# Conditioning sums as background steps, and the last layer's gates early

## The chip, the cores and the metric

The kernel runs on one core of a Trainium2 chip. TensorE (PE) multiplies matrices, VectorE (DVE), ScalarE (ACT) and GpSimd (POOL) work element by element, and SyncE (SP) issues the DMA transfers. The metric is the time of one launch in microseconds on the device, as the median of several runs. Before the change it is 1941.36 us.

## The reference

A first block of two layers works on 256 tokens `x` and 256 context tokens, each of width 1024; a second block (FFN, attention, FFN, twice) follows and isn't touched. In the first block each layer's conditioning comes from one vector per unit, `c` for the tokens and `c_ctx` for the context:

```python
def modulation(cond, w, b):
    m = jax.nn.silu(cond) @ w + b
    return jnp.split(m, 3, axis=-1)
...
        sh, sc, gt = modulation(c, ada_w[l], ada_b[l])
        shc, scc, gtc = modulation(c_ctx, ada_w[l], ada_b[l])
        h = rms_norm(x, norm_pre[l]) * (1.0 + sc[:, None]) + sh[:, None]
        hc = rms_norm(xc, norm_pre[l]) * (1.0 + scc) + shc

        z = h @ w_in[l]
        ...
        out = merge_branches(z, (y_a, y_b, y_c), w_branch[l], w_out[l])
        x_new = x + gt[:, None] * rms_norm(out, norm_post[l])
```

So a layer needs two vectors of 1024 at its start (shift and scale, the `mod` of the kernel) and one at its end (the gate `gt`). Each is a product of one row of 1024 with a matrix 1024 x 1024. `merge_branches` multiplies three branches (attention, a long convolution, a gated MLP) by gates and by `w_branch`, adds them, and multiplies the sum by `w_out`. The last layer updates only `x`.

## The kernel before

**Matmuls.** Every fp32 product is three matmuls of halves: ScalarE writes the rounded upper half `hi`, VectorE subtracts and writes the lower half `lo` (`split`, L109), and `mm3` (lines L138 to L140) or `mm3_T` (L214 to L216) adds hi x hi, hi x lo and lo x hi in a PSUM bank. Weights come in raw blocks of 1 MB, are split in pieces of 128 x 1024, and stand in a ring of four `hi` and four `lo` tiles (`wload`). `lin` makes products by token block, `linT` the transposed ones; the four banks of the tag `mm` take both.

**Conditioning.** `cond_cols(l, j, nu)` makes 512 of the 3072 conditioning numbers of a layer: it loads four blocks of 128 x 1024 of the transposed matrix `ada_t` (512 KB each) into tiles of the weight ring, and for each block and unit one `tensor_tensor_reduce` of VectorE (L350, called CUSTOM_DVE_ANT_0 in the trace and ISA in the order) multiplies it by the row of `crow` and adds along it; a small read of the accumulator follows. With two units a group of 512 has eight such reduces. L353 adds the bias. `ada_mod` (j = 0 to 3) writes the shift and scale of a layer, `ada_gate` (j = 4, 5) transposes the sums on TensorE (`tr<-ident,cond`, L222, four for each unit) and multiplies by `norm_post` (L373).

**The order of the work.** Instructions run in the order of the program on each engine, with priorities that move some ahead (`tc.high_priority`, `tc.issue_after`). Work of long latency (filters, convolution, attention heads) is written as generators in the list `bg`; `tick(ns)` inside the matmul loops runs one step of the first when the nanoseconds that the steps before asked for by their `yield` have passed, and `drain()` runs all that is left.

**A layer.** After the products of `w_in` come three merges, each in two halves of 512 columns: `merge(1)`, `merge(2)`, `merge(0)`. Each half forms its selection `sg`, pops one entry of `hooks`, then multiplies by `w_branch` and evacuates (`wb_evac`, L868 and L869). In layer 0 the six hooks are the four groups of layer 1's modulation (into `mod1`) and the two of layer 0's gate (into `gt`); in layer 1 the first four are empty and the last two are its own gate. `drain()` stands before `merge(2)`. A layer ends with `tail`: the product with `w_out` in two halves n of 512 columns. In layer 0 all four token blocks of half 0 come first, in layer 1 both halves of one token block. `ev` squares on ScalarE (L922) into `y` in the slot `s45`, multiplies by the gate on VectorE (L923), and after half 1 adds the normed result to the residual (L927). Then the next layer's, or FFN's, norm and transposes follow (L1041 for the scaling after layer 1).

Tiles with a tag have a fixed number of buffers; a new one waits until the readers of the old one are done. `slot(tag, ...)` has one buffer, `st` four, the ring's `hi` and `lo` four each.

Of the kernel before, what the change touches and what calls it, by code (L numbers as in the profile page):

```python
# [22 lines left out]
GAP = 2600.0  # L23
# [9 lines left out]
def model(ctx: ExitStack, tc: tile.TileContext, I, COL, out, dump=None):  # L33
# [193 lines left out]
    def rsqrt(a, b, eps, tag="rstd"):  # L227

        r = pool.tile([128, 1], F32, name=tag, tag=tag, bufs=6)
# [39 lines left out]
    def first():  # L269
# [70 lines left out]
        def cond_cols(l, j, nu):  # L340

            d = small(8, "cond").rearrange("p (b u) -> p b u", u=2)[:, :, :nu]
            for b in range(4):
                tag = ("hi", "lo")[b % 2]
                wt = wp.tile([128, 1024], F32, name=tag, tag=tag, bufs=4)
                n = (j * 4 + b) * 128
                SP.dma_start(wt, I["ada_t"][l][n:n + 128, :])
                for u in range(nu):
                    junk = pool.tile([128, 1024], BF16, name="w2", tag="w2", bufs=4)
                    DVE.tensor_tensor_reduce(junk, wt, crow[:, u, :], scale=0.5, scalar=0.0, op0=OP.mult, op1=OP.add,  # L350
                                             accum_out=d[:, b, u:u + 1])
            bias = col("ada_b", l)[:, j * 4:j * 4 + 4].unsqueeze(2).to_broadcast([128, 4, nu])
# [3 lines left out]
        def ada_mod(l, j, mod):  # L356
            d = cond_cols(l, j, 2)
            m = mod[:, j // 2, (j % 2) * 4:(j % 2) * 4 + 4, :]
            if j < 2:
                DVE.tensor_copy(m, d)  # L360
            else:
                g = col("norm_pre", l)[:, (j % 2) * 4:(j % 2) * 4 + 4]
                DVE.scalar_tensor_tensor(m, d, 1.0, g.unsqueeze(2).to_broadcast([128, 4, 2]), op0=OP.add, op1=OP.mult)

        def ada_gate(l, j, gt):

            nu = gt.shape[1]
            d = cond_cols(l, j, nu)
            npb = w2()
            SP.dma_start(npb, I["norm_post"][l:l + 1, (j - 4) * 512:(j - 3) * 512].partition_broadcast(128))  # L370
            for u in range(nu):
                ps = transpose4([d[:, b, u:u + 1].to_broadcast([128, 128]) for b in range(4)])
                DVE.tensor_tensor(gt[:, u, (j - 4) * 512:(j - 3) * 512], ps.rearrange("p a b -> p (a b)"), npb, op=OP.mult)  # L373
# [164 lines left out]
        def layer(l, hs, last, hooks, mid=None):  # L538

            W = I["w_in"][l]  # L540
            nu = 1 if last else 2
            T = 256 * nu
# [38 lines left out]
            def spectra():  # L581
# [3 lines left out]
                uT = slot("mg", [128, nu, 2, 2, 512], F32R)  # L585
# [188 lines left out]
            bg.append(heads())  # L774
# [43 lines left out]
            room = slot("mg", [128, 4, T + 128])  # L818
# [26 lines left out]
            mg = slot("mg", [128, 12 if last else 8, T])  # L845
# [49 lines left out]
            drain()  # L895
# [12 lines left out]
            merge(0, gh, gl, False, True)  # L908
# [74 lines left out]
        def later_rows():  # L983
            cond_rows()
            yield 0.0
        bg.append(later_rows())

        def mid0():
            rawalloc.extend(held)
# [451 lines left out]
```

## Time and profile before

| | us |
|---|---|
| median of 3 runs (lowest, highest) | 1941.36 (1939.37, 1943.46) |
| the profiled execution | 1942.45 |
| its span in the trace | 1940.3 |
| TensorE busy | 1900.5 (98%) |
| VectorE busy | 1234.5 (64%) |
| ScalarE busy | 973.4 (50%) |

The span is the stretch that the trace covers, and the profiled execution's time is a little longer. Busy time counts only instructions at work, so TensorE's 98% says that 40 us of the span are not covered by a matmul. [...]

### The profile page before, as it was taken

How to read it: one execution, taken by the hardware profiler on the slowest of the kernel's cores; microseconds unless marked ns; L12 is line 12 of the kernel's file. 1: busy time of each engine (PE TensorE's matmuls, PEld its weight loads, DVE VectorE, ACT ScalarE, POOL GpSimd, SP SyncE). 2: the span in 40 equal slices, each digit the busy share in tenths (PEclk: the TensorE clock that was granted, in tenths of full speed). 3: DMA queues.
4: the chain of work that ended last, by engine and by line, in shares of the span. 5: the costliest groups of instructions: out<-in, count | busy, mean ns of one | idle time of the engine just before them, and what ended most of it. 6: DMA issues, size and time to landing. Idle time of an engine off the chain costs nothing.

```text
span 1940.3 us, 27986 instructions
## 1 busy us (share of the span) xinstructions
PE 1900.5 (98%) x11280; PEld 1641.9 (85%) x11280; DVE 1234.5 (64%) x1862; ACT 973.4 (50%) x1536; POOL 81.0 (4%) x103
## 2 busy tenths in 40 slices
PE   6999999999999999999899999999999999999998
PEld 4788788778788888998799877799889988779996
DVE  4755667775877857657555578655565556875554
ACT  5534355552345457644444457644454445765443
POOL 0010100011000001010000000000000000000000
PEclk9999999999999999999899999999999999999999
DMA  8432323334552444457455554555655555454544
GB/s 292 156 110 77 100 79 131 117 114 150 185 186 93 145 138 134 146 179 280 167 177 172 185 177 138 174 192 172 197 192 186 163 187 175 149 195 152 180 158 141
DMA packets 155056, 312.29 MB, mean 161 GB/s; under 512 B 6126, under 2 KB 15920, under 8 KB 154800
## 3 DMA queue, kind: packets, MB, share of 16 engines
q1 hardware_dynamic: 153776, 306.33, 48.0%
q0 software_dynamic: 1152, 4.19, 0.7%
q8 instruction: 88, 1.44, 0.3%
q14 instruction: 40, 0.33, 0.0%
HBM read 309.45 MB, written 1.05 MB: 160 GB/s over the span
## 4 chain that ended last, share of the span: by engine, by line
PE 50%; DVE 2%; DMA 1%; ACT 1%; issue 0%; POOL 0%; POOLq 0%; ACTq 0%; DVEq 0%
PE mm L140 8%; PE mm L139 8%; PE mm L138 8%; PE mm L215 7%; PE mm L216 7%; PE mm L214 7%; PE tr L222 2%; DVE lo L110 1%; DMA raw<-in_ffn_w_gate 1%; PE po L1229 1%; PE aux L1196 0%; PE aux L1197 0%; ACT hi L110 0%; DMA raw<-in_w_out 0%; PE po L222 0%
## 5 line engine op out<-in xcount | busy, mean ns | idle before, releaser
L110 DVE TENSOR_TENSOR lo<-raw,hi 128x1024 fp32r<-128x1024 f32 (+1 forms) x484 | 575.2, 1193 | 455.0 <-ACT hi L110 449.6
L110 ACT ACTIVATE hi<-raw 128x1024 fp32r<-128x1024 f32 (+1 forms) x484 | 495.6, 1030 | 591.5 <-PE mm L215 307.1
L214 PE MATMUL mm<-H,hi 128*128 128x256 f32 (+1 forms) x2064 | 631.6, 306 | 2.7 <-ACT H L110 2.7
L215 PE MATMUL mm<-H,hi 128*128 128x256 f32 (+1 forms) x2064 | 629.1, 305 | 1.0 <-DVE H L110 1.0
L216 PE MATMUL mm<-H,lo 128*128 128x256 f32 (+1 forms) x2064 | 628.2, 304 | 0.0
L214 PEld LDWEIGHTS mm<-H,hi 128*128 128x128 f32 x2064 | 394.6, 191 | 20.8 <-ACT H L110 3.0
L215 PEld LDWEIGHTS mm<-H,hi 128*128 128x128 f32 x2064 | 394.8, 191 | 18.7 <-DVE H L110 1.9
L216 PEld LDWEIGHTS mm<-H,lo 128*128 128x128 f32 x2064 | 394.7, 191 | 16.7 <-issue 0.8
L138 PE MATMUL mm<-hi,H 128*128 128x512 f32 x576 | 228.4, 397 | 0.0
L140 PE MATMUL mm<-hi,H 128*128 128x512 f32 x576 | 226.7, 394 | 0.4 <-DVE H L110 0.4
L139 PE MATMUL mm<-lo,H 128*128 128x512 f32 x576 | 226.6, 394 | 0.0
L140 PEld LDWEIGHTS mm<-hi,H 128*128 128x128 f32 x576 | 108.9, 189 | 23.5 <-DVE H L110 1.1
L138 PEld LDWEIGHTS mm<-hi,H 128*128 128x128 f32 x576 | 108.9, 189 | 22.7 <-ACT pm L561 0.8
L139 PEld LDWEIGHTS mm<-lo,H 128*128 128x128 f32 x576 | 109.1, 189 | 22.2 <-issue 0.9
L138 PE MATMUL mm<-hi,s 128*128 128x512 f32 x192 | 75.4, 392 | 0.0
L139 PE MATMUL mm<-lo,s 128*128 128x512 f32 x192 | 75.3, 392 | 0.0
L140 PE MATMUL mm<-hi,s 128*128 128x512 f32 x192 | 75.0, 391 | 0.0
L138 PE MATMUL mm<-hi,mg 128*128 128x512 f32 x160 | 62.7, 392 | 0.0
L139 PE MATMUL mm<-lo,mg 128*128 128x512 f32 x160 | 62.6, 391 | 0.0
L140 PE MATMUL mm<-hi,mg 128*128 128x512 f32 x160 | 62.2, 391 | 0.0
L234 POOL TENSOR_TENSOR rstdb<-rstdb,mhalf 128x1 f32<-128x1 f32 x22 | 12.1, 548 | 1040.1 <-DVE rstdb L233 1040.1
L216 PE MATMUL mm<-s,lo 128*128 128x512 f32 (+1 forms) x128 | 47.1, 368 | 0.6 <-DVE lo L110 0.6
(387 smaller groups left out, 2410.9 us busy)
## 6 DMA issues: line engine op xcount, KB each, us to landing
raw<-in_w_in SPq DMA_DIRECT2D x68, 1024.0 KB, 5.3
raw<-in_ffn_w_gate SPq DMA_DIRECT2D x40, 1024.0 KB, 5.2
raw<-in_ffn_w_up SPq DMA_DIRECT2D x40, 1024.0 KB, 5.1
raw<-in_ffn_w_down SPq DMA_DIRECT2D x36, 1024.0 KB, 5.1
raw<-in_w_branch SPq DMA_DIRECT2D x12, 1024.0 KB, 5.1
raw<-in_a_w_qkv SPq DMA_DIRECT2D x12, 1024.0 KB, 5.2
hi<-in_ada_t SPq DMA_DIRECT2D x16, 512.0 KB, 3.8
lo<-in_ada_t SPq DMA_DIRECT2D x16, 512.0 KB, 5.6
```

Source lines behind the costliest of these rows:

```text
L110: last_split[:] = ACT.activation(hi, src, AF.Copy), DVE.tensor_tensor(lo, src, r32(hi), op=OP.subtract)
L138: PE.matmul(o, lhsT=xh, rhs=hi, start=start, stop=False)
L139: PE.matmul(o, lhsT=xh, rhs=lo, start=False, stop=False)
L140: last_mm[0] = PE.matmul(o, lhsT=xl, rhs=hi, start=False, stop=stop)
L214: PE.matmul(o, lhsT=wh, rhs=xh, start=start, stop=False, skip_group_check=skip)
L215: PE.matmul(o, lhsT=wh, rhs=xl, start=False, stop=False, skip_group_check=skip)
L216: last_mm[0] = PE.matmul(o, lhsT=wl, rhs=xh, start=False, stop=stop, skip_group_check=skip)
L222: PE.transpose(ps[:, i * 128:(i + 1) * 128], s, ident)
L234: powers.append(POOL.tensor_tensor(r, r, mhalf[:, :1], op=OP.pow))
L1229: PE.matmul(po[64 * m:64 * m + 64, i, :], lhsT=v[hf][:, b, (2 * i + m) * 64:(2 * i + m + 1) * 64], rhs=pT[t][:, i, m * (t + 1) + b, :], st ...
```

## The change

The conditioning functions become generators that yield after each block, and get their buffers from a function `place` in place of the ring. In layer 0 the rows of `crow` and the modulation of layer 1 are a background item behind the attention heads, in buffers of `st`; the gate of layer 0 is added to the background in the fifth hook, in four buffers of a tile in slot `s45`. Before `merge(2)` only the heads are run to their end; what is left is drained after `merge(0)`. In layer 1 the gate is a background item from the layer's start, in three buffers of the slot `mg`; its result stands in the fourth quarter of `mg` and is copied to its slot in the fifth hook. Line numbers of what follows grow by up to 21: L868, L869, L922, L923, L927 and L1041 become L881, L882, L937, L938, L942 and L1062, the reduce is L349 and the gate's product L376.

```diff
--- before.py
+++ after.py
@@ -226,7 +226,7 @@
 
     def rsqrt(a, b, eps, tag="rstd"):
 
-        r = pool.tile([128, 1], F32, name=tag, tag=tag, bufs=6)
+        r = pool.tile([128, 1], F32, name=tag, tag=tag, bufs=8 if tag == "rstdb" else 6)
         if b is None:
             DVE.tensor_scalar(r, a, eps, None, op0=OP.add)
         else:
@@ -337,40 +337,43 @@
                 ACT.activation(t, c, AF.Tanh, scale=0.5)
                 DVE.scalar_tensor_tensor(c, t, 1.0, c, op0=OP.add, op1=OP.mult)
 
-        def cond_cols(l, j, nu):
+        def cond_cols(l, j, nu, place):
 
             d = small(8, "cond").rearrange("p (b u) -> p b u", u=2)[:, :, :nu]
             for b in range(4):
-                tag = ("hi", "lo")[b % 2]
-                wt = wp.tile([128, 1024], F32, name=tag, tag=tag, bufs=4)
+                wt = place()
                 n = (j * 4 + b) * 128
                 SP.dma_start(wt, I["ada_t"][l][n:n + 128, :])
                 for u in range(nu):
                     junk = pool.tile([128, 1024], BF16, name="w2", tag="w2", bufs=4)
                     DVE.tensor_tensor_reduce(junk, wt, crow[:, u, :], scale=0.5, scalar=0.0, op0=OP.mult, op1=OP.add,
                                              accum_out=d[:, b, u:u + 1])
+                yield 2000.0 * nu
             bias = col("ada_b", l)[:, j * 4:j * 4 + 4].unsqueeze(2).to_broadcast([128, 4, nu])
             DVE.tensor_tensor(d, d, bias, op=OP.add)
             return d
 
-        def ada_mod(l, j, mod):
-            d = cond_cols(l, j, 2)
-            m = mod[:, j // 2, (j % 2) * 4:(j % 2) * 4 + 4, :]
-            if j < 2:
-                DVE.tensor_copy(m, d)
-            else:
-                g = col("norm_pre", l)[:, (j % 2) * 4:(j % 2) * 4 + 4]
-                DVE.scalar_tensor_tensor(m, d, 1.0, g.unsqueeze(2).to_broadcast([128, 4, 2]), op0=OP.add, op1=OP.mult)
-
-        def ada_gate(l, j, gt):
+        def ada_mod(l, mod, place):
+            for j in range(4):
+                d = yield from cond_cols(l, j, 2, place)
+                m = mod[:, j // 2, (j % 2) * 4:(j % 2) * 4 + 4, :]
+                if j < 2:
+                    DVE.tensor_copy(m, d)
+                else:
+                    g = col("norm_pre", l)[:, (j % 2) * 4:(j % 2) * 4 + 4]
+                    DVE.scalar_tensor_tensor(m, d, 1.0, g.unsqueeze(2).to_broadcast([128, 4, 2]), op0=OP.add, op1=OP.mult)
+
+        def ada_gate(l, gt, place):
 
             nu = gt.shape[1]
-            d = cond_cols(l, j, nu)
-            npb = w2()
-            SP.dma_start(npb, I["norm_post"][l:l + 1, (j - 4) * 512:(j - 3) * 512].partition_broadcast(128))
-            for u in range(nu):
-                ps = transpose4([d[:, b, u:u + 1].to_broadcast([128, 128]) for b in range(4)])
-                DVE.tensor_tensor(gt[:, u, (j - 4) * 512:(j - 3) * 512], ps.rearrange("p a b -> p (a b)"), npb, op=OP.mult)
+            for j in (4, 5):
+                d = yield from cond_cols(l, j, nu, place)
+                npb = w2()
+                SP.dma_start(npb, I["norm_post"][l:l + 1, (j - 4) * 512:(j - 3) * 512].partition_broadcast(128))
+                yield GAP
+                for u in range(nu):
+                    ps = transpose4([d[:, b, u:u + 1].to_broadcast([128, 128]) for b in range(4)])
+                    DVE.tensor_tensor(gt[:, u, (j - 4) * 512:(j - 3) * 512], ps.rearrange("p a b -> p (a b)"), npb, op=OP.mult)
 
         def reduced_sin(a, n, ps, b, f):
 
@@ -535,10 +538,17 @@
 
         spec = []
 
-        def layer(l, hs, last, hooks, mid=None):
+        def layer(l, hs, last, hooks, mid=None, beside=None):
 
             W = I["w_in"][l]
             nu = 1 if last else 2
+
+            def mgslot(shape):
+                if not last:
+                    return slot("mg", shape)
+                names = "abcd"[:len(shape) - 1]
+                return mgx[0][:, :math.prod(shape[1:])].rearrange(
+                    f"p ({' '.join(names)}) -> p {' '.join(names)}", **dict(zip(names, shape[1:])))
             T = 256 * nu
             movs = [(0, 256, unit_T(hs[0]))] if last else [(0, 512, lambda kb: (H[:, :, 0, kb, :], H[:, :, 1, kb, :]))]
             toks = [unit_tok(h, t) for h in hs[:nu] for t in range(2)]
@@ -582,7 +592,7 @@
 
 
                 D, G, Ksp, K256, rk = spec
-                uT = slot("mg", [128, nu, 2, 2, 512], F32R)
+                uT = slot("s8" if last else "mg", [128, nu, 2, 2, 512], F32R)
                 eos = []
                 for u in range(nu):
                     front, back = u_[:, :, u * 256:u * 256 + 128], u_[:, :, u * 256 + 128:(u + 1) * 256][:, :, ::-1]
@@ -771,7 +781,10 @@
                         yield gap
                     if n + 1 < len(units) and units[n + 1][0] != units[n][0]:
                         yield from stack(units[n + 1][0])
-            bg.append(heads())
+            heads_ = heads()
+            bg.append(heads_)
+            if beside:
+                bg.append(beside())
 
 
             if not last:
@@ -815,7 +828,7 @@
                 DVE.scalar_tensor_tensor(g, g, r, lnb, op0=OP.mult, op1=OP.add)
             lin(W, 8, CGM + 512, 512, toks, gv_evac)
 
-            room = slot("mg", [128, 4, T + 128])
+            room = mgslot([128, 4, T + 128])
             uu, bt = room[:, :, :T], room[:, :, T:]
             for i in range(2):
                 SP.dma_start(bt[i * 64:(i + 1) * 64], I["gm_bs"][l].rearrange("(b i) q -> i b q", i=2)[i:i + 1].partition_broadcast(64))
@@ -842,7 +855,7 @@
             zT(CGC, gc_evac)
 
 
-            mg = slot("mg", [128, 12 if last else 8, T])
+            mg = mgslot([128, 12 if last else 8, T])
             later = []
 
             def merge(i, gh, gl, first_, last_):
@@ -892,7 +905,8 @@
             for b in range(4):
                 split(gh[:, b, :], gl[:, b, :], gB[:, b, :])
             merge(1, gh, gl, True, False)
-            drain()
+            while heads_ in bg:
+                step()
             gh, gl = gpair(1)
             for b in range(4):
                 split(*[g[:, b, :].rearrange("p (t q) -> p t q", q=128) for g in (gh, gl)], vb[:, b])
@@ -906,6 +920,7 @@
             for b in range(4):
                 split(gh[:, b, :], gl[:, b, :], on[0][:, b, :])
             merge(0, gh, gl, False, True)
+            drain()
             return [H[:, u] for u in range(nu)]
 
         def tail(l, hm, gt, res, done):
@@ -980,11 +995,6 @@
         modulate(xh[1], mod0, 1, hs[1], 0)
         bg.append(hyena_filter(0))
 
-        def later_rows():
-            cond_rows()
-            yield 0.0
-        bg.append(later_rows())
-
         def mid0():
             rawalloc.extend(held)
             raws = [rawload(I["ada_w"][0], k0, 4, j * 512, 512) for j in (1, 3) for k0 in (0, 4)]
@@ -997,15 +1007,21 @@
                 modulate(xh[u], mod0, u, hs[u], 4)
         mid = mid0, mid1, [(u * 256, 256, unit_T(h)) for u, h in enumerate(hs)]
         rope = pool.tile([128, 2, 2, 64], F32, name="rope", tag="rope")
-        gt = []
-
-        def gt0(j):
-            if j == 4:
-                list(hyena_filter(1))
-                gt.append(slot("s2", [128, 2, 1024]))
-            ada_gate(0, j, gt[0])
-        hooks = [lambda j=j: ada_mod(1, j, mod1) for j in range(4)] + [lambda j=j: gt0(j) for j in (4, 5)]
-        hm = layer(0, hs, False, hooks, mid)
+        gt, mgx = [], []
+
+        def beside0():
+            cond_rows()
+            yield 3 * GAP
+            yield from ada_mod(1, mod1, lambda: st([128, 1024], F32))
+
+        def gt0():
+            list(hyena_filter(1))
+            gt.append(slot("s2", [128, 2, 1024]))
+            room = slot("s45", [128, 4, 1024])
+            places = iter([room[:, i, :] for i in range(4)] * 2)
+            bg.append(ada_gate(0, gt[0], lambda: next(places)))
+        hooks = [lambda: None] * 4 + [gt0]
+        hm = layer(0, hs, False, hooks, mid, beside0)
         xs = xtile()
         SP.dma_start(xs, xin)
         res = [xs, slot("s7", [128, 2, 1024])]
@@ -1018,12 +1034,17 @@
         dump("xs0", xs)
         gt.clear()
 
-        def gt1(j):
-            if j == 4:
-                gt.append(slot("s2", [128, 1, 1024]))
-            ada_gate(1, j, gt[0])
-        hooks = [lambda: None] * 4 + [lambda j=j: gt1(j) for j in (4, 5)]
-        hm = layer(1, hs, True, hooks)
+
+        mgx.append(slot("mg", [128, 4096]))
+        early_gt = mgx[0][:, 3072:].rearrange("p (u d) -> p u d", u=1)
+        room = mgx[0].rearrange("p (i k) -> p i k", k=1024)
+        places1 = iter([room[:, i % 3, :] for i in range(8)])
+        bg.append(ada_gate(1, early_gt, lambda: next(places1)))
+
+        def gt1():
+            gt.append(slot("s2", [128, 1, 1024]))
+            ACT.activation(gt[0], early_gt, AF.Copy)
+        hm = layer(1, hs, True, [lambda: None] * 4 + [gt1])
         g1 = slot("s8", [128, 1024])
         SP.dma_start(g1, I["ffn1_norm_2"][0:1].partition_broadcast(128))
         then = norm_to_h(xs, g1)
```

**VectorE at layer 0's end.** The rows go from the last evacuations of `merge(0)` to w_out's first. `lo`, `wl`, `mg` and the numbered `s` written by L110 are lower halves of weights, `H` those of the merged rows, `mm` is a PSUM bank. Before:

```order
L868 SCALAR_TENSOR_TENSOR s_4290<-s_4290,mm 128x512
L869 TENSOR_TENSOR mg<-mg,s_4290 128x512 x2
L110 TENSOR_TENSOR lo<-raw,hi 128x1024
L110 TENSOR_TENSOR H<-mg,H 128x256 x7
L110 TENSOR_TENSOR mg<-raw,mg 128x1024 x2
L110 TENSOR_TENSOR s_4567<-raw,s_4567 128x1024
L110 TENSOR_TENSOR wl<-raw,wh 128x1024
L110 TENSOR_TENSOR lo<-raw,hi 128x1024 x3
L923 TENSOR_TENSOR s_4565<-mm,s_4179 128x512 x4
```

Now the beginning of the same stretch, from the last L881:

```order
L881 SCALAR_TENSOR_TENSOR s_4222<-s_4222,mm 128x512
L110 TENSOR_TENSOR lo<-raw,hi 128x1024
L882 TENSOR_TENSOR mg<-mg,s_4222 128x512
L110 TENSOR_TENSOR H<-mg,H 128x256 x8
L353 TENSOR_TENSOR cond<-cond,cols 128x8
L349 ISA w_4266,cond<-st,crow 128x1024
L349 ISA cond 128x1
L110 TENSOR_TENSOR mg<-raw,mg 128x1024 x2
L110 TENSOR_TENSOR s_4560<-raw,s_4560 128x1024
L110 TENSOR_TENSOR wl<-raw,wh 128x1024
L364 SCALAR_TENSOR_TENSOR mod<-cond,cols 128x8
L349 ISA w_4268,cond<-st,crow 128x1024
```

and its end, up to the first evacuations of w_out (here `s_4139` is the tile of the gate's blocks and `s_4138` the gate):

```order
L349 ISA w_4531,cond<-s_4139,crow 128x1024
L349 ISA cond 128x1
L349 ISA w_4533,cond<-s_4139,crow 128x1024
L349 ISA cond 128x1
L353 TENSOR_TENSOR cond<-cond,cols 128x8
L938 TENSOR_TENSOR s_4558<-mm,s_4138 128x512 x4
L376 TENSOR_TENSOR s_4138<-tr,w_4536 128x512 x2
```

From L881 to the first L938 there are 24 reduces now (8 for the modulation, 16 for the gate), nine lower halves of weights, eight of `H` and two gate products; before, no reduce stands there.

**TensorE at the same place.** The transposes of the gate's sums are `tr<-ident,cond`. Before they stand among the products of `w_branch`, four at a time:

```order
L215 MATMUL mm<-s_3916,hi 128x512
L222 MATMUL tr<-ident,cond 128x128 x4
L216 MATMUL mm<-s_3915,lo 128x512
L214 MATMUL mm<-s_3915,hi 128x512
L215 MATMUL mm<-s_3916,hi 128x512
L216 MATMUL mm<-s_3915,lo 128x512
```

Now they stand between w_out's half 0 (weights `hi`, `lo`) and its half 1 (weights in `mg`):

```order
L138 MATMUL mm<-hi,H 128x512
L139 MATMUL mm<-lo,H 128x512
L140 MATMUL mm<-hi,H 128x512
L222 MATMUL tr<-ident,cond 128x128 x12
L138 MATMUL mm<-mg,H 128x512
L139 MATMUL mm<-mg,H 128x512
L140 MATMUL mm<-mg,H 128x512
```

Twelve of the sixteen transposes moved to this place; the last four come eight products later.

**VectorE at layer 1's end.** `s_8076` (now `s_8061`) is `y`, `xs` the residual. Before:

```order
L923 TENSOR_TENSOR s_8076<-mm,s_7763 128x512
L110 TENSOR_TENSOR lo<-raw,hi 128x1024 x2
L923 TENSOR_TENSOR s_8076<-mm,s_7763 128x512
L233 SCALAR_TENSOR_TENSOR rstd<-small 128x1
L927 SCALAR_TENSOR_TENSOR xs<-s_8076,rstd,xs 128x512
L110 TENSOR_TENSOR lo<-raw,hi 128x1024 x2
L923 TENSOR_TENSOR s_8076<-mm,s_7763 128x512 x2
L233 SCALAR_TENSOR_TENSOR rstd<-small 128x1
L927 SCALAR_TENSOR_TENSOR xs<-s_8076,rstd,xs 128x512 x3
```

Now:

```order
L938 TENSOR_TENSOR s_8061<-mm,s_7799 128x512 x2
L233 SCALAR_TENSOR_TENSOR rstd<-small 128x1
L942 SCALAR_TENSOR_TENSOR xs<-s_8061,rstd,xs 128x512
L110 TENSOR_TENSOR lo<-raw,hi 128x1024 x4
L942 SCALAR_TENSOR_TENSOR xs<-s_8061,rstd,xs 128x512
L938 TENSOR_TENSOR s_8061<-mm,s_7799 128x512
L233 SCALAR_TENSOR_TENSOR rstdb<-small 128x1
L1062 SCALAR_TENSOR_TENSOR w_8167<-xs,rstdb,s_8057 128x512
L1062 SCALAR_TENSOR_TENSOR w_8168<-xs,rstdb,s_8057 128x512
L938 TENSOR_TENSOR s_8061<-mm,s_7799 128x512
```

The second half of token block 0's residual and its two scalings (L1062) moved ahead of the last evacuation of token block 1.

## Rows read from the trace of the kernel before

**Rows 1.** The page: span, busy time, and loads of ada_t with us to landing.
```profile
span 1940.3 us, 27986 instructions
...
PE 1900.5 (98%) x11280; PEld 1641.9 (85%) x11280; DVE 1234.5 (64%) x1862; ACT 973.4 (50%) x1536; POOL 81.0 (4%) x103
...
hi<-in_ada_t SPq DMA_DIRECT2D x16, 512.0 KB, 3.8
lo<-in_ada_t SPq DMA_DIRECT2D x16, 512.0 KB, 5.6
```
**Rows 2.** Busy time by stretch: stretch, its us, busy us of each engine, clock.
```profile
core 0: us, PE busy (x) PEld busy (x) DVE busy (x) ACT busy (x) POOL busy (x), PEclk, DMA share, GB/s
567.34:588.94 21.60, 21.60 (x97) 17.86 (x96) 15.38 (x22) 11.29 (x18) 0.00 (x0) 1.00 0.70 231
...
613.22:665.00 51.78, 51.40 (x329) 46.55 (x328) 41.44 (x78) 28.91 (x54) 3.65 (x4) 1.00 0.37 120
...
880.00:904.00 24.00, 22.59 (x187) 22.13 (x186) 21.35 (x31) 10.12 (x12) 0.00 (x0) 1.00 0.80 286
904.00:927.62 23.62, 22.69 (x96) 17.40 (x94) 17.64 (x22) 12.72 (x20) 0.55 (x1) 1.00 0.75 244
927.62:933.19 5.57, 0.00 (x1) 0.01 (x1) 4.33 (x10) 2.79 (x8) 1.54 (x2) 0.83 1.00 358
933.19:942.82 9.63, 9.25 (x28) 6.95 (x29) 3.29 (x6) 1.20 (x2) 0.55 (x1) 0.57 0.04 14
942.82:952.00 9.18, 9.18 (x46) 7.72 (x45) 4.79 (x5) 7.37 (x9) 0.00 (x0) 1.00 0.05 8
```
**Rows 3.** VectorE's groups in w_out's half 0 of layer 0: busy us, mean ns.
```profile
L110 DVE TENSOR_TENSOR lo<-raw,hi 128x1024 fp32r<-128x1024 f32 x4 | 4.8, 1222 | 3.9 <-ACT hi L110 3.9
L110 DVE TENSOR_TENSOR H<-mg,H 128x256 fp32r<-128x256 f32 x8 | 2.8, 417 | 0.0
...
L923 DVE TENSOR_TENSOR s<-mm,s 128x512 f32<-128x512 f32 x3 | 2.0, 685 | 0.2 <-ACT s L922 0.2
```
**Rows 4.** TensorE's timeline, halves 0 and 1 of w_out: start us, us, instruction.
```profile
588.71 0.39 PE L140 MATMUL mm<-hi,H 128*128 128x512 f32 x1
588.94 0.39 PE L138 MATMUL mm<-mg,H 128*128 128x512 f32 x1
```
**Rows 5.** VectorE's timeline, the last evacuation of layer 0's last merge.
```profile
567.40 0.68 DVE L868 SCALAR_TENSOR_TENSOR s<-s,mm 128x512 f32<-128x512 f32 x1
```
**Rows 6.** VectorE's timeline, reduces of layer 1's gate.
```profile
893.03 1.23 DVE L350 CUSTOM_DVE_ANT_0 w<-hi,crow 128x1024 bf16<-128x1024 f32 x1 [1.41 <-DMA hi<-in_ada_t]
...
894.30 1.23 DVE L350 CUSTOM_DVE_ANT_0 w<-lo,crow 128x1024 bf16<-128x1024 f32 x1
...
895.45 2.36 DVE L110 TENSOR_TENSOR lo<-raw,hi 128x1024 fp32r<-128x1024 f32 x2
897.72 1.22 DVE L350 CUSTOM_DVE_ANT_0 w<-hi,crow 128x1024 bf16<-128x1024 f32 x1
...
898.87 1.22 DVE L350 CUSTOM_DVE_ANT_0 w<-lo,crow 128x1024 bf16<-128x1024 f32 x1
```
**Rows 7.** TensorE's waits from 870 to 960: us in total, times, longest.
```profile
PE tr L222 <- DVE w L1041: 5.6, 1, 5.6
PE tr L222 <- DVE cond L353: 0.8, 1, 0.8
```
**Rows 8.** TensorE's timeline, products behind the hole at layer 1's end.
```profile
937.19 0.63 PE L138 MATMUL mm<-hi,H 128*128 128x512 f32 x1
...
941.46 0.43 PE L139 MATMUL mm<-lo,H 128*128 128x512 f32 x1
```
**Rows 9.** VectorE's timeline, layer 1's end: evacuations and residual halves.
```profile
927.56 1.51 DVE L923 TENSOR_TENSOR s<-mm,s 128x512 f32<-128x512 f32 x2
...
929.05 0.74 DVE L927 SCALAR_TENSOR_TENSOR xs<-s,rstd,xs 128x512 f32<-128x512 f32 x1
```
**Rows 10.** ScalarE's timeline, a square of w_out's result.
```profile
921.69 0.58 ACT L922 ACTIVATE s<-mm 128x512 f32<-128x512 f32 x1
```

## The prediction

> **What bounds the kernel now.** I read the page's busy part first: TensorE is busy 1900.5 of 1940.3 us and VectorE two thirds of that, so a change of VectorE's work pays or costs only where TensorE stands still for it [rows 1]. Then I read busy time stretch by stretch for the five places the change touches [rows 2]. In layer 0's w_out stage (567.34 to 588.94, the products of output half 0) TensorE is busy 21.60 of 21.60 us and VectorE only 15.38. Layer 1's opening (613.22 to 665.00) leaves VectorE 10.3 us free. Layer 1's last merge and its w_out lose 1.41 and 0.93 us. [...] TensorE's waits name the causes: 5.6 us for VectorE's normed rows, 0.8 us for the gate's sums [rows 7].
>
> **Layer 0: the reduces meet the end of the layer.** Before, layer 0's 48 reduces (24 blocks of ada_t, two units each) were done in the hooks, ahead of the last merge's evacuations; the order has the last of them ahead of the row of L868. Now they are background steps behind the attention heads, two per step, and the rest is drained after merge(0). In VectorE's new order 24 of the 48 stand between the merge's last evacuation (L881) and w_out's first (L938). TensorE can't go round them: 12 transposes of gate sums stand between its two halves of w_out, and the last four of these need the sum (L353) that stands right behind reduce 24. So half 1 waits for that whole queue.
>
> Its start and its content: the last product of the merge is out when VectorE starts L868 at 567.40 [rows 5]; half 1 of w_out starts at 588.94 [rows 4], so 21.5 us are covered.
> - 24 reduces: one takes 1.22 to 1.23 us, and the next starts 1.15 us (897.72 to 898.87) to 1.27 us (893.03 to 894.30) after it [rows 6]. I take 1.2: 28.8 us (27.6 to 30.5).
> - 9 lower halves of weights (128x1024), one more than the eight that stand there before: 1.22 each [rows 3], a little less in a row, as two took 2.36 at 895.45 [rows 6]: 9 x 1.18 = 10.6 us (10.3 to 11.0).
> - 8 lower halves of H (128x256): 2.8 us [rows 3].
> - The merge's L881 and L882 and two gate products L376, at 0.68 as L868 takes [rows 5]: 2.7 us. Four bias sums and two mod rows, tiny: 0.7 us, an estimate.
>
> That is 45.6 us. Behind the last reduce ScalarE can write its squares, since y lies in the slot (s45) in which the gate's blocks were: 0.58 us for L937, which was L922 before [rows 10], then 0.69 for the first scaled evacuation, L938, before L923 [rows 3]. With that, 46.9. The blocks come through four buffers, each loaded once its reduces are done, between weight loads on the same queue; a load of 512 KB took 3.8 to 5.6 us from issue to landing [rows 1]. Most of that lies beside the weight halves; I add 2, for 49 us. Half 1 then starts at 567.4 + 49 = 616.4 in place of 588.94: **+27.5 us**. Lower end: the short spacings and no load or square on the path, 43.7, +22. Upper end: the long spacings and 4 us of loads, 53.5, +32. The cover that the 24 reduces would have needed is VectorE's idle time in the stage, 21.60 - 15.38 = 6.2 us, good for five.
>
> After the 5.57 us hole at layer 1's end the next 9.63 us ran at a mean granted clock of 0.57, so 9.63 x 0.43 = 4.1 us of work was not done [rows 2]; the matmuls there came 0.43 us apart (937.19 to 941.46, ten intervals) against 0.23 at the full clock [rows 8, 4]. Behind some 27 us of waiting I take the same, **+4** (0, if the transposes that trickle in keep the clock, to 10, if a second hole follows: the three other token blocks are evacuated by the same engine).
>
> **Layer 0's hooks.** The merges lose their 24 blocks of work and w_out's weights get the ring: TensorE's share there was already full, and the only wait there is short. **-0.5** (0 to -1.5).
>
> **Layer 1: gates early.** The 8 reduces, two bias sums and gate products, some 10 to 11 us of VectorE, move from the last merge to the layer's first stage, which has 10.3 us free of 51.78 [rows 2]. They are steps of one block, and the loads go into mg, which is empty then. What may wait is the eight transposes, now in the zT products. As the cover is just used up, **+1** (0 to +4, if three or four evacuations each wait for one reduce). The copy of the gate from mg into its slot is ScalarE's, half busy there; nothing.
>
> What is removed at the other end: the ada_t loads out of the hi and lo ring, which held up w_out's weights. The idle of 880 to 927.62 is 1.41 + 0.93 = 2.34 us [rows 2], 0.82 of it for the gate's sum [rows 7]: **-2.3** (0 to -3).
>
> **Layer 1's end.** Before, VectorE's order puts both evacuations of token block 1 (927.56) ahead of token block 0's second half of the residual (929.05) [rows 9]; the norm of block 0 so ends after the last product of w_out, and nothing is left for TensorE. In the new order that second half stands four rows ahead of block 1's last evacuation, behind four weight halves, and the norm's rows stand ahead of it too. From 927.62 to 942.82 15.2 us passed with 8 transposes and 16 or so products and 4 more transposes, about 5.2 us of work at the full rate: the hole costs 10.0 with its clock. The chain of block 0 (which took 5.6 us from 927.56 on, block 1's evacuations in it) now can run beside block 1's products, 24 of them behind each evacuation; I expect 2 us of wait left and no fall of the clock: **-8** (-3, if the weight halves still hold it, to -10).
>
> **Sum.** +27.5 + 4 - 0.5 + 1 - 2.3 - 8 = +21.7. The profiled execution took 1942.45 (span 1940.3 and 2.15 around it), 1.1 above the median of the runs, 1941.36; it so becomes 1964.2 and the median **1963**.
>
> **The rivals.**
> - *The reduces don't hold TensorE* (other side). VectorE takes w_out's evacuations past the waiting reduces, or the gate's sums are ready by 588.94, so that the layer ends as before; then 1941.36 - 0.5 + 1 - 2.3 - 8 = 1932. It decides from where the queue is under 21.6 us, that is, at most five reduces on top of 15.4 us, or 0.25 us a reduce in place of 1.2. For it: VectorE is idle 6.2 us there. Against it: block 0's residual half began at 929.05, when block 1's two evacuations that stand ahead of it in the order were through (927.56 and 1.51 us) [rows 9]. [...] Chance 0.05.
> - *The clock stays low and layer 1's end gains nothing*: +27.5 + 10 - 0.5 + 4 - 2.3 = +38.7, 1980. For it: the 9.63 us at 0.57 after a far shorter hole, and the four weight halves still ahead of block 0's second half. Against it: full clock again from 942.82 on [rows 2]. Chance 0.09.
> - *A third of the wait is covered*: TensorE waits only for the sums of the gate's first half, 16 reduces in, and the 8 behind them (9.6 us) run beside half 1, with no fall of the clock: +17.9 - 0.5 + 1 - 2.3 - 8 = +8.1, 1949. Against it: the last four of the twelve transposes, of the gate's second half, stand in TensorE's order ahead of half 1 too. Chance 0.07.
>
> **How the numbers follow.** The forecast has 0.79. All low ends together give 1949, all high ends 1984; 1949 to 1977 leaves out the first two rivals and the corner. A measurement of this kernel tells about 0.2%, 3.9 us, from no change. Faster is the first rival, 0.04 of it; within 0.2%, what is left of it and the lower edge of the third, 0.03; slower 0.93.
>
> **What would show it.** In the new profile: TensorE's largest wait is one of 22 to 32 us for L353, around 589, with VectorE's reduces back to back through it; a low granted clock right behind it; the hole at layer 1's end a third as long or less, with a granted clock of 1.00; no wait of transposes in the last merge. I am wrong if TensorE runs through 589 without that wait, or if a hole of 5 us stands at layer 1's end still.

## The result and the profile after

The changed kernel takes 1958.24 us (median of 4, 1957.19 to 1961.82), against 1941.45 before beside it: a ratio of 1.0089 (95% interval 1.0076 to 1.0102), 16.8 us slower. The page after, which answers to [rows 1]:

```profile
span 1955.8 us, 27995 instructions
...
PE 1898.7 (97%) x11280; PEld 1642.7 (84%) x11280; DVE 1237.8 (63%) x1862; ACT 981.3 (50%) x1539; POOL 85.1 (4%) x103
```

TensorE is busy 1.8 us less than before (1900.5), the other engines 3 to 8 us more; the 15.5 us of span are time in which TensorE waits. To see where, I compared the start of the same product of a layer in both traces, counting the products that go into the banks `mm` (9860 in each trace; background products aren't counted, so a shift in mid-layer also holds what background work has moved).

| the product | start before | start after | shift | step |
|---|---|---|---|---|
| layer 0, behind the first spectra | 228.9 | 223.7 | -5.2 | -5.2 |
| w_out half 0, layer 0 | 567.2 | 559.2 | -8.0 | -2.7 |
| w_out half 1 | 588.9 | 607.0 | +18.0 | +26.0 |
| 60 products on | 603.6 | 623.1 | +19.6 | +1.5 |
| layer 1, before the last merge's second half | 881.3 | 909.7 | +28.4 | +8.8 |
| in w_out, layer 1 | 910.1 | 936.0 | +25.9 | -2.5 |
| early in FFN | 945.8 | 962.3 | +16.5 | -9.4 |
| end of the span | 1940.3 | 1955.8 | +15.5 | -1.0 |

**Layer 0's end.** TensorE's timeline after, between the halves of w_out (start, us, instruction, in brackets the idle time before it and what ended it), answers to [rows 4]:

```profile
596.16 1.12 PE L222 MATMUL tr<-ident,cond 128*128 128x128 f32 x4 [15.05 <-DVE cond L353]
599.05 1.12 PE L222 MATMUL tr<-ident,cond 128*128 128x128 f32 x4 [1.78 <-DVE s L376]
605.82 1.09 PE L222 MATMUL tr<-ident,cond 128*128 128x128 f32 x4 [5.65 <-DVE cond L353]
606.98 0.79 PE L138 MATMUL mm<-mg,H 128*128 128x512 f32 x1
```

The one long wait is three, 22.5 us in all: two end with sums of the gate (L353), one with a gate product (L376), which reads the bank of the four transposes before. VectorE's timeline of the same stretch, against [rows 5, 6]:

```profile
560.67 0.68 DVE L881 SCALAR_TENSOR_TENSOR s<-s,mm 128x512 f32<-128x512 f32 x1
...
586.70 1.22 DVE L349 CUSTOM_DVE_ANT_0 w<-s,crow 128x1024 bf16<-128x1024 f32 x1
...
587.92 1.22 DVE L349 CUSTOM_DVE_ANT_0 w<-s,crow 128x1024 bf16<-128x1024 f32 x1
589.07 1.22 DVE L349 CUSTOM_DVE_ANT_0 w<-s,crow 128x1024 bf16<-128x1024 f32 x1
...
605.51 0.17 DVE L353 TENSOR_TENSOR cond<-cond,cols 128x8 f32<-128x8 f32 x1
606.23 2.48 DVE L938 TENSOR_TENSOR s<-mm,s 128x512 f32<-128x512 f32 x4 [0.55 <-ACT s L937]
```

From the last L881 to half 1 the queue takes 46.3 us. It also begins 1.3 us later behind half 0's first product than before (560.67 against 559.2; before, 567.40 against 567.2), and so 46.3 us of queue make 26.0 us of shift. Reduces follow each other at 1.15 us (587.92 to 589.07) with hardly a gap. The busy time by stretch shows the same (columns as in [rows 2]; PEclk is the clock that TensorE was granted, as a share of the full one):

```profile
559.40:580.95 21.55, 21.55 (x96) 17.64 (x94) 20.39 (x34) 10.31 (x16) 0.00 (x0) 1.00 0.75 268
580.95:606.98 26.03, 3.48 (x14) 2.16 (x13) 25.37 (x49) 2.53 (x6) 0.00 (x0) 0.58 0.49 162
606.98:623.13 16.15, 16.15 (x72) 13.36 (x73) 8.30 (x17) 4.23 (x13) 1.64 (x3) 0.93 0.01 1
...
672.33:702.39 30.06, 26.50 (x115) 21.34 (x114) 24.35 (x37) 9.55 (x12) 3.36 (x2) 0.94 0.45 146
...
953.50:962.32 8.82, 8.75 (x43) 6.43 (x41) 6.31 (x12) 4.44 (x9) 1.10 (x2) 1.00 0.47 172
```

VectorE is busy 25.37 of the 26.03 us in which TensorE does 3.48 us of work, and the clock is low in the wait (0.58) and a little behind it (0.93).

**Layer 1.** TensorE's waits over the whole span, against [rows 7]:

```profile
PE tr L222 <- DVE cond L353: 21.0, 3, 15.1
...
PE mm L138 <- DVE s L684: 3.6, 1, 3.6
...
PE tr L222 <- DVE w L1062: 1.3, 1, 1.3
```

A new wait of 3.6 us (L684 evacuates the products for the keys) is followed by low clock, the 0.94 of the row 672.33 above. From the product at 603.6 (before) to that at 881.3 the busy times are, before and after:

```profile
603.57:881.34 277.77, 275.66 (x1953) 255.82 (x1952) 195.24 (x320) 160.92 (x278) 23.93 (x25) 1.00 0.44 145
623.14:909.73 286.59, 278.94 (x1961) 257.49 (x1960) 207.24 (x336) 164.05 (x280) 24.41 (x25) 0.99 0.46 154
```

So 5.5 of the 8.8 us are waiting (TensorE stands still 7.65 us in place of 2.11). Of the 3.3 us that it is busy longer, about 1.8 are the low clock (30.06 us at 0.94) and 0.9 the eight transposes of the gate, which now stand here (0.11 us each: behind four of them, at 664.11, the product of 664.80 starts 0.46 us later than the spacing of 0.23 us around it would have it). The hole of 5.6 us at the layer's end [rows 7, 9] is 1.3 now, and the clock behind it stays at 1.00 in the row 953.50. VectorE's timeline there shows the new order: the second residual half, the norm and the scaling of block 0 ahead of block 1's last evacuation.

```profile
949.82 0.74 DVE L942 SCALAR_TENSOR_TENSOR xs<-s,rstd,xs 128x512 f32<-128x512 f32 x1
950.49 0.68 DVE L938 TENSOR_TENSOR s<-mm,s 128x512 f32<-128x512 f32 x1
...
952.17 1.41 DVE L1062 SCALAR_TENSOR_TENSOR w<-xs,rstdb,s 128x512 f32<-128x512 f32 x2 [0.66 <-POOL rstdb L234]
953.51 0.68 DVE L938 TENSOR_TENSOR s<-mm,s 128x512 f32<-128x512 f32 x1
```

### The profile page after: what moved, and what is told of

It is laid out like the page before. It is cut to its first block, busy times and chain, and to the rows that moved or that the text cites. A ratio compares the mean times of both kernels' runs of the same rounds, so it can differ in the third digit from the quotient of the medians.

```text
span 1955.8 us, 27995 instructions
## 1 busy us (share of the span) xinstructions
PE 1898.7 (97%) x11280; PEld 1642.7 (84%) x11280; DVE 1237.8 (63%) x1862; ACT 981.3 (50%) x1539; POOL 85.1 (4%) x103
## 4 chain that ended last, share of the span: by engine, by line
PE 86%; DVE 7%; DMA 3%; ACT 2%; issue 1%; POOL 1%; POOLq 0%; SPq 0%; ACTq 0%; DVEq 0%
PE mm L214 15%; PE mm L215 15%; PE mm L216 15%; PE mm L138 10%; PE mm L140 10%; PE mm L139 10%; PE tr L222 3%; DVE lo L110 2%; DVE w L349 2%; ACT hi L110 1%; PE po L1250 1%; PE po L752 1%; PE aux L728 1%; DMA raw<-in_w_in 1%; PE po L222 1%
## 5 line engine op out<-in xcount | busy, mean ns | idle before, releaser
L110 DVE TENSOR_TENSOR lo<-raw,hi 128x1024 fp32r<-128x1024 f32 (+1 forms) x484 | 574.7, 1192 | 466.7 <-ACT hi L110 464.8
L110 ACT ACTIVATE hi<-raw 128x1024 fp32r<-128x1024 f32 (+1 forms) x484 | 496.2, 1030 | 572.6 <-PE mm L215 343.9
L216 PEld LDWEIGHTS mm<-H,lo 128*128 128x128 f32 x2064 | 394.6, 191 | 16.5 <-issue 0.8
L214 PE MATMUL mm<-s,hi 128*128 128x512 f32 (+1 forms) x128 | 47.2, 369 | 0.0
```

Of the source, the lines that this page charges most:

```text
L110: last_split[:] = ACT.activation(hi, src, AF.Copy), DVE.tensor_tensor(lo, src, r32(hi), op=OP.subtract)
L214: PE.matmul(o, lhsT=wh, rhs=xh, start=start, stop=False, skip_group_check=skip)
L216: last_mm[0] = PE.matmul(o, lhsT=wl, rhs=xh, start=False, stop=stop, skip_group_check=skip)
```

## The experiments

Ratios are against the kernel before, run beside each kernel on the same chip; its medians were 1943.1 us (experiments 1 to 4), 1941.62 (5 to 8) and 1942.51 (9 to 12). A shift is read from one trace of each kernel. At 171 us, where the kernels hardly differ yet, the shifts of the thirteen traces lie between -1.5 and +1.0 us; a shift is good to about that.

**1 and 2. Each half of the change alone.** In the first, layer 1's gate goes back to the last merge and the ring; in the second, layer 0's work goes back to the hooks, and the rows of `crow` to the background item behind the first filter.

```diff
-        bg.append(ada_gate(1, early_gt, lambda: next(places1)))
+        list(ada_gate(1, gt[0], ring(), (j,)))            # in hooks 4 and 5 of layer 1
```
```diff
-        hooks = [lambda: None] * 4 + [gt0]
-        hm = layer(0, hs, False, hooks, mid, beside0)
+        hooks = [lambda j=j: list(ada_mod(1, mod1, ring(), (j,))) for j in range(4)] + [lambda j=j: gt0(j) for j in (4, 5)]
+        hm = layer(0, hs, False, hooks, mid)
```

> Layer 0 of the change alone; layer 1's gate is made in the last merge as before. Theory: the two halves of the change add up. By the starts of the same products in the two traces layer 0 gives back 8.0 us before w_out and loses 27.6 in it, so 1941.4 + 19.6 = 1961 us (1958 to 1964), and the hole of 5.6 us at layer 1's end is there again. Rival, the sizes of the prediction: +27.5 + 4 - 0.5 = +31, 1972 us; then the changed kernel would owe more to layer 1.

> Layer 1's early gate alone; layer 0 as before. Theory: layer 1's start and body lose 8.8 us as they do in the changed kernel, the last merge wins 2.1 to 2.5, the hole at the end 9.4: -2.7 to -3.1, 1938.5 us (1936 to 1941), with a wait of some 3.6 us for L684. Rival, the sizes of the prediction (+1 - 2.3 - 8): 1932 us; then the 8.8 us belong to layer 0, which hands its late end on.

Layer 0 alone: 1961.11 us, ratio 1.0096 (1.0081 to 1.0112), 18.0 slower. Its starts shift by -7.7 before w_out and +27.1 through it, and the hole is back:

```profile
PE tr L222 <- DVE cond L353: 21.0, 4, 14.2
...
PE tr L222 <- DVE w L1065: 5.6, 1, 5.6
PE mm L214 <- ACT H L110: 2.7, 1, 2.7
PE mm L138 <- ACT mg L110: 2.3, 1, 2.3
```

Layer 1 alone: 1940.21, ratio 0.9985 (0.9976 to 0.9995), 2.9 faster; it loses 8.5 us in the layer's body and has the wait before L684 (L692 there, 3.7 us). The two differences add up to +15.1, the whole change measured +16.8. The sizes of the table of starts hold, the prediction's for layer 1 (-9.3) don't.

**3 and 4. The dose.** Only the price of a step in layer 0 changes, and with it how many reduces VectorE's order has between the last merge's evacuation and w_out's first: 24 at 2000, 18 at 1500, none at 1000.

```diff
-                yield 2000.0 * nu
+                yield 1000.0 * nu if nu == 2 else 2000.0      # the other run: 1500.0
```

> The changed kernel with a smaller cost per step in layer 0 (1500 in place of 2000 for each unit), so that steps come more often; VectorE's order then has 18 reduces between the last merge's evacuation and w_out's first in place of 24. Theory (the queue of reduces is the wait): six reduces at 1.15 us less, 1958.2 - 6.9 = 1951 us (1949 to 1954), the waits for the gate's sums 14 us in place of 21. Rival (the loads of the blocks or the transposes hold it): as many loads and transposes, 1958 us.

> As the run before with 1000 for each unit: no reduce is left in that queue. Theory: the 26.0 us and the 1.5 us of low clock behind them go, less some 2 us for gate transposes that move back among the merge's products: 1933 us (1930 to 1938). Rival (VectorE is too full for 48 reduces beside the merges, wherever they stand): TensorE waits for evacuations in the merges instead, and the time stays above 1945 us.

18 reduces: 1950.84 us, ratio 1.0046 (1.0031 to 1.0061), 7.4 faster than the changed kernel's median (6.9 expected for six reduces). Half 1 lost 17.7 us in place of 26.0, and the waits for the gate at this place (TensorE's waits, 560 to 630) are 14.2 in place of 22.5:

```profile
PE tr L222 <- DVE cond L353: 12.4, 2, 6.6
PE tr L222 <- DVE s L376: 1.8, 1, 1.8
```

No reduce: 1936.17, ratio 0.9962 (0.9949 to 0.9975), 6.9 faster than before (1933 expected; the rival's 1945 falls), and no wait for L353 is left at this place: from half 0 to half 1 (554.16 to 584.60) TensorE is busy 30.28 of 30.44 us, with gate transposes and background products of the next filter in between:

```profile
554.16:584.60 30.44, 30.28 (x141) 23.82 (x140) 21.55 (x33) 16.13 (x27) 2.70 (x4) 1.00 0.67 225
```

The loads were as many in all three kernels, and twelve gate transposes stand between the halves in each; the queue of reduces is the cause. (This trace is of an execution of 1931.37 us, 4.8 below the median of its kernel.)

**5. Where layer 0's early gain comes from.** Layer 1's early gate, the reduces of layer 0 in the hooks, and only the rows of `crow` made later.

```diff
-        bg.append(later_rows())
...
-        hm = layer(0, hs, False, hooks, mid)
+        hm = layer(0, hs, False, hooks, mid, cond_rows)       # called where the heads are queued
```

> Layer 1's early gate as in the run of it alone, and in layer 0 one thing more: the rows of crow are made behind the convolution stage, as in the changed kernel, and not in the background item behind the first filter; the 48 reduces stay in the hooks. Theory: the 4.1 us that the changed kernel wins between 197 and 229 us are this move, which takes the wait of 2.5 us for L614 away; so 3.7 to 4 us below layer 1 alone, 6.6 to 7 below before, 1936 us. Rival (that stretch is won by the reduces' leaving): as layer 1 alone, 3 below before, 1940 us.

1935.88, ratio 0.9973 (0.9963 to 0.9982), 5.7 faster than before and so 2.8 more than layer 1 alone. Between the starts 171 and 229 it wins 3.6 us, and the wait that stands there in layer 1 alone, as in the kernel before (L614 there), is gone; the line is of layer 1 alone:

```profile
PE aux L138 <- DVE w L632: 2.5, 1, 2.5
```

So the first 3 to 4 us are the rows of `crow`, which the prediction didn't price.

**6 to 9. Layer 1's body.** All have steps of 1000 in layer 0. The loss is the shift of the starts from 647.0 to 881.3 us (the expectations count 6.1 from 603.6 on). The run with steps of 1000 lost 5.5 us there, but in a trace 4.8 us below its median; the five other kernels with the same layer 1 lost 7.5 to 8.7 in theirs. The edits: fewer reduces (two in place of eight, which leaves layer 1's gate incomplete); steps at 200 ns; the gate behind the convolution; and the last two together.

```diff
+                if nu == 1 and b == 0:
+                    DVE.memset(d, 0.0)
-                for u in range(nu):
+                for u in range(nu if nu == 2 or b == 0 else 0):
```
```diff
-                yield 1000.0 * nu if nu == 2 else 2000.0
+                yield 1000.0 * nu if nu == 2 else 200.0       # likewise the GAP of the gate
```
```diff
             bg.append(conv_)
+            if last:
+                bg.append(mgx[1])                             # layer 1's gate
...
+            while last and mgx[1] in bg:
+                step()
             room = mgslot([128, 4, T + 128])
```

> The kernel with steps of 1000, with only the first block of each half of layer 1's gate reduced, so two reduces in place of eight (loads, steps and transposes stay; the gate of layer 1 is left incomplete). It lost 6.1 us in layer 1's body against before. Theory (the reduces stand in VectorE's order ahead of evacuations there): the wait for L684 goes and the loss falls to 1 to 2 us, so some 4.5 us faster than with all eight, 11 to 12 us below before. Rival (the steps of the gate take their turn from convolution and heads, which then come late): no difference, 7 us below before.

> The same kernel with all eight reduces, but the gate's steps in layer 1 ask for 200 ns each in place of 2000 or 2600, so that convolution and heads start some 20 us of matmuls earlier. Theory (the reduces cost the time): same loss or 1 to 3 us more, since they come closer together: 4 to 7 us below before. Rival (the steps take their turn): the loss goes, 11 to 12 us below before.

> The same kernel with layer 1's gate as a background item behind the convolution and ahead of the heads, and run to its end before the slot mg is written. Theory (reduces): VectorE's full stage is spared, no wait for L684, 10 to 12 us below before. Rival (steps): the heads are as late as before and end in a rush, 6 to 8 us below before.

> The last run but with the gate's steps in layer 1 asking for 200 ns each: behind the convolution, ahead of the heads, and nearly free. Both causes should so be met: the reduces stand in a stage where VectorE has room, and the heads start some 20 us of matmuls earlier than with the full price. Theory (each of the two costs about 4 us, and either alone leaves the other): layer 1's body loses 1 to 2 us in place of 4.4, so 13 to 14 us below before, 1928 us. Rival (eight reduces in a row make a wait of their own wherever they stand): 9 to 11 below, as with the full price.

| | us | ratio | loss in layer 1's body |
|---|---|---|---|
| few reduces | 1931.62 | 0.9948 (0.9931 to 0.9965) | 4.8 |
| steps at 200 ns | 1933.99 | 0.9956 (0.9941 to 0.9971) | 5.7 |
| behind the convolution | 1931.72 | 0.9945 (0.9930 to 0.9959) | 4.4 |
| behind, at 200 ns | 1930.56 | 0.9942 (0.9927 to 0.9956) | 3.1 |

By the medians they are 10.0, 7.6, 9.9 and 12.0 us faster than before; with steps of 1000 alone it was 6.9. Their intervals overlap with that one's, so the single steps between them are partly argued from the traces.

Neither theory holds alone. With two reduces the wait for L684 goes and the kernel wins some 3 us, not the 4.5 expected; the heads still come late, and a loss of 4.8 stays. Behind the first stage (677.8 to 881.3 us of the table) TensorE stands still 1.6 us before, 3.5 in the changed kernel and 1.5 with cheap steps: that is the price of late heads. With cheap steps nothing is lost behind the first stage (the shift of the starts is +5.0 at 667 us and +5.3 at 881), but the whole loss is in that stage, where the reduces stand close together:

```profile
PE mm L138 <- ACT w L570: 3.4, 1, 3.4
```

That is not VectorE's evacuation but ScalarE's L570, which copies a bank for the short convolution into a work tile. The view of the reduces' line says that ScalarE waited for them:

```profile
L349 DVE CUSTOM_DVE_ANT_0 w<-mg,crow x8: 1221/1226/1227, 636.8 to 652.3; 128x1024 bf16<-128x1024 f32 x8
...
  ACT w L570: 13.3, 2
```

The copy reads nothing that a reduce makes. But a reduce writes its products, which nobody reads, into a tile of the same tag (`w2`, four buffers) as the convolution's copy. So a reduce that waits in the queue also holds a buffer that ScalarE needs. With both remedies 3.1 us are left, more than the 1 to 2 expected; 0.9 of it are the eight gate transposes that moved here (0.11 us each). Most of the other 2 is waiting too: over layer 1's body TensorE stands still 3.9 us there, 1.7 more than before, nearly all of it among the heads. What makes the heads wait I haven't settled.

**10 and 11. Layer 0 again, beside the best layer 1.** Modulation and gate in the hooks and the ring; or the gate alone in the background.

```diff
-        hooks = [lambda: None] * 4 + [gt0]
+        hooks = [lambda j=j: list(ada_mod(1, mod1, ring(), (j,))) for j in range(4)] + [gt0]     # the first run: gate in hooks 4, 5 too
```

> Layer 1 as in the run before; layer 0 with its 48 reduces in the hooks and the weight ring as before the change, only the rows of crow made behind the convolution stage. Theory: in layer 0 the background steps win nothing over the hooks once they are off w_out's path (-4.1 against -2.8 to -4.5 at the end of w_out in the runs so far), so within 2 us of the run before, 13 to 14 below before. Rival (the ring's freedom is worth something in layer 0): 3 us or more slower than the run before.

> Layer 1 as in the two runs before; in layer 0 the modulation in the hooks and only the gate in the background, in the slot s45 from the fifth hook on. VectorE's order has all reduces ahead of the last merge's evacuations. Theory: as the run before within 2 us, 12 to 15 below before. Rival (16 reduces in the last merge hold its evacuations): a new wait there, 5 us or more slower than the run before.

1928.73, ratio 0.9934 (0.9917 to 0.9951), and 1927.49, ratio 0.9925 (0.9911 to 0.9940). The second, 15.0 us faster than before, is the best version; the intervals don't part the two from each other. So in layer 0 the background steps win nothing over the hooks, and both rivals (3 and 5 us slower than the run before) fall. All its waits from 500 to 965 are short:

```profile
PE tr L222 <- DVE w L1069: 1.3, 1, 1.3
PE tr L222 <- DVE sqd L769: 1.0, 2, 0.6
```

**12. Six reduces, and a miss.** The changed kernel with the gate of layer 0 back in the hooks.

```diff
-            bg.append(ada_gate(0, gt[0], lambda: next(places)))
+            list(ada_gate(0, gt[0], ring(), (j,)))            # in hooks 4 and 5 of layer 0
```

> The changed kernel with layer 0's gate back in the hooks and the ring, so that only modulation is in the background: VectorE's order has 6 reduces between the last merge's evacuation and w_out's first, in place of 24, and no transpose stands between the halves of w_out. Theory (queue against cover): the queue is 18 x 1.15 = 20.7 us shorter than the 47.3 measured, 26.6 against a cover of 21.5, so half 1 still waits, but 5 us; 20 us faster than the changed kernel, 4 us below before, 1938 us. Rival (the transposes are what holds half 1): no wait there at all, 9 us below before.

1950.1, ratio 1.0041 (1.0026 to 1.0056), 12 us slower than expected. Half 1 doesn't wait at all: from the last merge evacuation (561.51) to w_out's first (581.63) the queue takes 20.1 us, less than the cover of 21.5, so my 5 us were too much. (The 47.3 of the expectation is 46.3 by the rows above.) That is also what the rival said of half 1, so this run doesn't part the two there; the run without a reduce does, with its transposes in place and no wait. But I had counted only the reduces ahead of w_out's first evacuation. Twelve more stand behind its fourth, among the residuals:

```profile
583.97 1.28 DVE L946 TENSOR_TENSOR s<-mm,s 128x512 f32<-128x512 f32 x2
...
589.73 0.16 DVE L233 SCALAR_TENSOR_TENSOR rstd<-small 128x1 f32<-128x1 f32 x1
589.80 1.22 DVE L349 CUSTOM_DVE_ANT_0 w<-st,crow 128x1024 bf16<-128x1024 f32 x1
...
603.77 0.75 DVE L950 SCALAR_TENSOR_TENSOR s<-s,rstd,s 128x512 f32<-128x512 f32 x1 [0.43 <-POOL rstd L234]
```

so layer 1's norm is late, and TensorE waits for it at the layer's start (waits from 590 to 640):

```profile
PE tr L222 <- DVE pm L512: 4.5, 1, 4.5
PE po L222 <- DVE pm L512: 2.6, 1, 2.6
PE po L222 <- ACT w L524: 1.9, 1, 1.9
PE mm L214 <- ACT H L110: 1.7, 1, 1.7
```

The same products of layer 1 shift by 18.1 us there (from -8.4 to +9.8) and by 2.2 more behind it, at a low clock: each four transposes take 1.09 to 1.12 us from 612.42 to 620.14 on, against 0.65 at 605.79, and the products of 128x256 from 624.10 to 627.94 come 0.21 us apart, against 0.12 in the trace of before (901.13 to 902.08). The queue was moved behind the place that I counted to, not shortened.

## Why the prediction was right

The predicted 1963 stands against 1958.24. The sum by its terms:

- **Half 1 waits for the queue, +27.5:** 26.0 measured. VectorE's queue took 46.3 us against 49, and began 1.3 us later. The reduces came at the short spacing of [rows 6], 1.15 us, throughout, and the 2 us for loads were not needed. The dose of 24, 18 and 0 reduces shows that they are the cause: 26.0, 17.7 and no wait. Two bounds of the sum don't add up: its own terms give 44.1 us for the shortest queue and 53.0 for the longest, in place of 43.7 and 53.5; the range moves by 0.5 us at most.
- **The clock behind it, +4:** 1.5. The granted clock fell, to 0.58, but mostly while TensorE was waiting for VectorE anyway; only 16 us at 0.93 came behind it.
- **Layer 0's hooks, -0.5:** the step failed. Up to w_out the kernel wins 8.0, some 4 of it by the later rows of `crow`, which have no term in the sum; with them the wait for L614 goes. Some 1.8 us (0.11 each) are the sixteen gate transposes that moved behind that point, twelve of them into the 26.0. The rest I didn't take apart.
- **Layer 1's early gate, +1:** 8.8; this step failed too. I compared 10 us of reduces with 10 us of idle time in the stage. The runs show two costs beside each other: evacuations and ScalarE's copies wait for the reduces in the order (a wait of 3.6 us and about 1.8 of low clock behind it), and the gate's steps take their turn from the heads, which then come late (some 2 us of waiting). The upper bound of +4 was too low.
- **The ring, -2.3:** -2.5. **Layer 1's end, -8:** -9.4, with a wait of 1.3 us and no fall of the clock.

So the direction and the main term were right for the reason given. That the total came within 5 us is luck: two missed sizes, 7.5 us too little gain and 7.8 too little loss, cancel. The first rival falls: the trace of after shows L938 behind all 24 reduces. None of w_out's evacuations passed a waiting reduce: the first of them ran at 606.23, the last sum of the gate at 605.51. The second and third fall with the table of starts. Of the signs that I named, the wait was there, in three parts, the longest 15.05 us; the clock behind it was low for 2 us only (products 0.43 us apart at 608.42, 0.23 from 609.26 on); the hole at layer 1's end fell to a quarter, at full clock; and the last merge has no wait of transposes.

## What to carry to other kernels

Background work that wasn't done by the end of the merges was drained here at the worst place. So count, on the engine that does it, what stands between the last result of one stage and the first evacuation of the next, and go on counting to the end of that stage, and compare it in microseconds with the matmul time that covers it. A price for a step that is set too high (2000 ns for a reduce of 1.15 us) leaves work for the drain; here half that price turned 16.8 us of loss into 6.9 of gain. Idle time of an engine in a stage was no room here for work that stood in its queue ahead of evacuations: with 10.3 us of it in layer 1's opening [rows 2], TensorE waited 3.6 us for L684. And a scratch output holds buffers too; with steps at 200 ns ScalarE's copies waited 13.3 us for reduces.

## What the hardware showed beside that

Two of the early reduces took almost twice as long as the others. VectorE's timeline after:

```profile
672.20 2.34 DVE L349 CUSTOM_DVE_ANT_0 w<-mg,crow 128x1024 bf16<-128x1024 f32 x1
...
674.47 2.30 DVE L349 CUSTOM_DVE_ANT_0 w<-mg,crow 128x1024 bf16<-128x1024 f32 x1
...
678.51 1.21 DVE L349 CUSTOM_DVE_ANT_0 w<-mg,crow 128x1024 bf16<-128x1024 f32 x1
```

and GpSimd's in the same stretch:

```profile
672.16 3.53 POOL L601 TENSOR_TENSOR st<-s 128x512 f32<-128x512 f32 x2 [31.80 <-DVE s L588]
```

GpSimd's two additions took 3.53 us; before, 2.57 (at 644.49, beside a VectorE idle for all but the first 0.5 us). In the first run with steps of 200 ns, at 428.69 and 430.92 in layer 0, two reduces took 2.30 and 2.31 us beside four additions of GpSimd (423.14, 9.00 us), and the next, at 433.16 behind them, 1.22. So these four reduces took 1.1 us more than others. But a reduce at 424.38 in the trace of after took 1.22 us beside four such additions (422.21, 8.02 us): what makes the difference isn't shown.
